# A two-layer mixer on one core: 128-column token sums at the start, wider lead groups with the last one's modulation on VectorE, and token-major last output columns

## The chip, the core and the metric

The kernel runs on one NeuronCore of one Trainium2 chip. The metric is the time of one launch on the device, in microseconds (us), as the median of several runs; lower is better. The engines are called PE (TensorE, the matrix engine), DVE (VectorE), ACT (ScalarE), POOL (GpSimd) and SP (SyncE, which here only issues DMAs). All of a core's engines run their own instruction streams in order and wait for one another through semaphores.

## The reference, cut to what matters

Context tokens (128) and sample tokens (256) go through two layers and a final norm. `cvec` is one conditioning vector for the context tokens and another for the sample tokens.

```python
def trunk_layer(x, cvec, l, p, ...):
    shift, scale, gate = jnp.split(jax.nn.silu(cvec) @ p['w_mod'][l] + p['b_mod'][l], 3, axis=-1)
    h = rmsnorm(x, p['norm_g'][l]) * (1 + scale) + shift
    (f_x, f_g, p_x, p_g, q, k, v, a_g, c_a, c_b, c_g) = jnp.split(h @ p['w_in'][l], 11, axis=-1)
    ...                                   # four mixers, each multiplied by silu of its gate
    y = jnp.concatenate([y_f, y_p, y_a, y_c], axis=-1) @ p['w_out'][l]
    return x + gate * y, k, v
y = rmsnorm(x, final_g)                   # after the second layer
```

`x` has 384 tokens of 2048 channels; `w_mod[l]` is 2048 x 6144, `w_in[l]` 2048 x 5632, `w_out[l]` 2048 x 2048, all in fp32.

## The kernel before

**Layout.** Activations stand channel-major: 16 blocks of 128 channels on the partitions, 384 tokens along the free dimension. Every large product is made of three single-pass products (`mm3`, lines 439 to 442): the weight and the activation are each split into a rounded part and a rest (`hi`, `lo` of a weight tile; `hh`, `hl` of `h`; `yh`, `yl` of the mixers' output), and hi x hi, hi x rest and rest x hi are added in PSUM. `wtile` (line 227) loads a weight tile `raw` by DMA (512 KB for two channel blocks and 512 output columns), copies it rounded to `hi` on ACT and subtracts to `lo` on DVE.

**The start.** Three dummy products (`idle`, line 167) on a zero tile `still` stand ahead. The tokens' sums of squares over all channels come from `token_sums` (line 421): the squared channels are the stationary operand and one column of ones is the moving one. From the sums come 1/rms (`rstd_cols`), its diagonal, and a broadcast product `bc`; from `h`'s scale and shift (`AB`) and `bc`, `make_h` (line 427) makes a channel block of `h` with four DVE and two ACT instructions. The scale and shift are the product of `silu(cvec)` with columns of `w_mod`; `mod_item` (line 255) does it on PE, with the two conditioning vectors as stationary operand in 32 columns (`cmod`), four column strips side by side, from 512 KB tiles `mraw` in the pool `Y`.

**The lead phase.** `h` isn't ready at once, so four of layer 0's input chunks (`C_B`, `C_A`, `K_`, `Q_`, 512 columns each) run group by group over the channel blocks: `groups` are two of one block and seven of two. Within a group each of the four chunks takes all four PSUM tiles of the pool `mmp`, runs `main_tile` (24 products of 384 columns for two blocks) and leaves a partial result, which DVE adds to `acc[ci]` in four instructions (helper `tt`, line 107); the next chunk on PE needs those PSUM tiles back. The modulation of the next group (`mod_group`, eight `mod_item`s) is put ahead of the first and the third chunk, and `make_h` for the next group ahead of the fourth. PE and SP follow the written order throughout this phase, DVE and ACT the order that the scheduler makes.

**The end.** In layer 1, `w_out` is applied for four groups of 512 output channels. `finish_block` (line 914) adds gate times result to `x`, squares it and adds the squares to `sacc`. The first three groups are multiplied by `final_g`, transposed to token-major on PE and copied to `ot`. The fourth group runs one block of 128 channels at a time; only after its last block are the token sums complete, 1/rms known, and twelve tiles of 128 tokens x 512 channels scaled and stored.

Of the kernel before, what the change touches and what calls it, by code (L numbers as in the profile page):

```python
# [8 lines left out]
F32 = mybir.dt.float32  # L9
# [5 lines left out]
P = 128  # L15
# [40 lines left out]
def mixer_step(  # L56
    ctx: ExitStack,
    tc: tile.TileContext,
    x_in, cache_k, cache_v, consts, lam, packs,
# [76 lines left out]
    nc.vector.memset(still, 0.0)  # L136
# [3 lines left out]
    nc.vector.memset(cmod, 0.0)  # L140

# [17 lines left out]
    act(warm, cmod[:, 0, 2:3], AF.Sqrt, bias=eps_t[:, 0:1])  # L159
# [183 lines left out]

    fill = {"pe": [], "dve": []}
# [76 lines left out]
    def token_sums(st, acc, start=True, stop=True):  # L421
        for t in range(TB):
            nc.tensor.matmul(st[:, t:t + 1], lhsT=acc[:, t * P:(t + 1) * P], rhs=ones[:, 0:1], start=start and t == 0,  # L423
                             stop=stop and t == TB - 1)
        return st[:, 0:TB]
# [358 lines left out]
    for l in range(DEPTH):  # L784
        if l == 0:
            groups = [(0, 1), (1, 1)] + [(k, 2) for k in range(2, KC, 2)]
            first = mod_group(0, *groups[0])
            ssq = sm("ssq")
            for g in range(4):
                if g == 3:  # L790
                    for it in first[:2]:
                        mod_item(*it)
                for i in range(2):
                    stat = token_sums(ssq, xsq[g][:, i, :], g == 0 and i == 0, g == 3 and i == 1)
            dg = diagonal(rstd_cols(stat, TB, 1.0 / D))
# [8 lines left out]
        hh = [gtile("H", "hh", dt=F32R) for _ in range(4)]  # L804
        hl = [gtile("H", "hl", dt=F32R) for _ in range(4)]
        res = {}
        if l == 0:
# [106 lines left out]
        def finish_block(g, b, ps, outs):  # L914
# [18 lines left out]
        otk = []  # L933
        for g in range(4):
            ps4 = [mmp.tile([P, 512], F32, tag="mm", name=nm("mm")) for _ in range(4)]
# [6 lines left out]
            for b in range(4):  # L942
                if g == 3:
                    c0 = g * BR + b * P
                    for k0 in range(0, KC, 8):
# [6 lines left out]
                        if b == 3 and k0 == 0:  # L952
                            tots.append(mdp.tile([P, 512], F32, tag="md", name=nm("st")) if final else sm("st"))
# [4 lines left out]
            elif g < 3:  # L958
# [147 lines left out]
```

## Time and profile before

| | us |
|---|---|
| median of 3 runs | 1249.11 |
| runs | 1248.88 to 1251.1 |
| the profiled execution, its time | 1249.6 |
| the profiled execution, its span | 1247.8 |
| mean granted PE clock (share of full speed) | 0.986 |

The span runs from the first to the last recorded instruction; 1.8 us of the profiled time lie around it. Shares of busy time are averages over stages; the rows further down are read stage by stage. All times in rows are us from the span's start unless marked ns.

### The profile page before, as it was taken

Reading aid. Unit: us, or ns where it says so; the run is one execution under the profiler, and the core shown is the slowest. Engines: PE = TensorE matmul, PEld = TensorE weight load, DVE = VectorE, ACT = ScalarE, POOL = GpSimd, SP = SyncE. Lnnn points to the kernel's source line nnn. Section 1 sums busy time; section 2 is a strip of 40 time slices with the busy share of each in tenths; the row PEclk is TensorE's granted clock in tenths of the full one; section 3 lists DMA queues with packets and bytes.
Section 4 is the critical chain, followed back from the end, with each engine's and each line's share of the span. In section 5 each row is a group of like instructions: output and inputs, shape, how many; then the busy total and the mean of one; then the engine's idle time right before and its main releaser. Section 6 shows DMA issues by size and latency. Waiting matters only on the chain.

```text
span 1247.8 us, 22061 instructions
## 1 busy us (share of the span) xinstructions
PE 1223.0 (98%) x8558; PEld 1148.6 (92%) x8558; DVE 922.4 (74%) x1774; ACT 550.3 (44%) x1103; POOL 2.1 (0%) x34
## 2 busy tenths in 40 slices
PE   8999999999999999999999999999999999999995
PEld 6899998898999999999998999989999999999995
DVE  4787879999957956989968469997464895647452
ACT  3433333444547644433335433334455755344442
POOL 0000000000000000000000000000000000000000
PEclk6999999999999999999999999999999999999998
DMA  8988886553346766988945444444232563645322
GB/s 302 351 314 318 304 306 236 171 175 122 132 169 218 281 228 221 330 302 319 326 155 185 161 152 161 152 163 156 80 101 102 194 228 118 211 152 186 119 68 101
DMA packets 70712, 251.85 MB, mean 202 GB/s; under 512 B 7760, under 2 KB 8912, under 8 KB 70608
## 3 DMA queue, kind: packets, MB, share of 16 engines
q1 hardware_dynamic: 70608, 250.45, 57.1%
q8 instruction: 67, 1.10, 0.4%
q14 instruction: 37, 0.30, 0.1%
HBM read 243.08 MB, written 7.34 MB: 201 GB/s over the span
## 4 chain that ended last, share of the span: by engine, by line
PE 91%; DVE 5%; DMA 1%; ACT 1%; issue 1%; SPq 0%; DVEq 0%; ACTq 0%
PE mm L440 24%; PE mm L442 23%; PE mm L441 23%; PE mod L279 5%; PE mm L471 2%; PE mm L472 2%; PE mm L473 2%; DVE lo L107 1%; PE sp L440 1%; PE sp L441 1%; PE sp L442 1%; DVE cacc L110 1%; PE fb L712 1%; PE ssq L423 1%; PE aso L669 1%
## 5 line engine op out<-in xcount | busy, mean ns | idle before, releaser
L116 ACT ACTIVATE hi<-raw 128x512 fp32r<-128x512 f32 x498 | 308.9, 631 | 532.6 <-PE mm L441 345.8
L107 DVE TENSOR_TENSOR lo<-raw,hi 128x512 fp32r<-128x512 f32 x498 | 336.8, 688 | 212.7 <-ACT hi L116 203.6
L440 PE MATMUL mm<-hh,hi 128*128 128x384 f32 x1280 | 441.0, 345 | 3.7 <-ACT hh L113 3.7
L442 PE MATMUL mm<-hh,lo 128*128 128x384 f32 x1280 | 433.0, 338 | 2.5 <-DVE lo L107 2.5
L441 PE MATMUL mm<-hl,hi 128*128 128x384 f32 x1280 | 433.0, 338 | 0.0
L440 PEld LDWEIGHTS mm<-hh,hi 128*128 128x128 f32 x1280 | 242.0, 189 | 23.6 <-issue 10.1
L442 PEld LDWEIGHTS mm<-hh,lo 128*128 128x128 f32 x1280 | 242.3, 189 | 3.5 <-DVE lo L107 3.4
L441 PEld LDWEIGHTS mm<-hl,hi 128*128 128x128 f32 x1280 | 242.4, 189 | 1.0 <-DVE hl L110 0.4
L440 PE MATMUL mm<-yh,hi 128*128 128x384 f32 x512 | 173.6, 341 | 0.6 <-DVE xr L110 0.6
L441 PE MATMUL mm<-yl,hi 128*128 128x384 f32 x512 | 172.6, 337 | 0.0
L442 PE MATMUL mm<-yh,lo 128*128 128x384 f32 x512 | 172.5, 338 | 0.0
L110 DVE SCALAR_TENSOR_TENSOR macc<-sraw,cmod,macc 128x512 f32<-128x512 f32 x210 | 147.6, 746 | 6.3 <-DMA sraw<-in_w_mod_dram 6.3
L110 DVE SCALAR_TENSOR_TENSOR cacc<-u,cst,cacc 128x399 f32<-128x399 f32 x232 | 146.5, 631 | 6.0 <-ACT cacc L113 1.5
L440 PEld LDWEIGHTS mm<-yh,hi 128*128 128x128 f32 x512 | 96.4, 188 | 4.1 <-issue 2.5
L441 PEld LDWEIGHTS mm<-yl,hi 128*128 128x128 f32 x512 | 96.5, 188 | 0.0
L442 PEld LDWEIGHTS mm<-yh,lo 128*128 128x128 f32 x512 | 96.4, 188 | 0.0
L107 DVE TENSOR_TENSOR acc<-acc,mm 128x384 f32<-128x384 f32 x128 | 66.5, 553 | 26.9 <-PE mm L442 26.6
L279 PE MATMUL mod<-mraw,cmod 128*32 128x128 f32 (+2 forms) x1920 | 74.7, 296 | 0.0
L279 PEld LDWEIGHTS mod<-mraw,cmod 128*32 128x32 f32 x1920 | 49.7, 114 | 18.5 <-issue 10.6
L113 ACT ACTIVATE hh<-ht,AB 128x128 fp32r<-128x128 f32 x64 | 27.2, 451 | 27.5 <-DVE ht L110 26.8
L471 PE MATMUL mm<-hi,hh 128*128 128x512 f32 x96 | 38.3, 399 | 0.0
L472 PE MATMUL mm<-lo,hh 128*128 128x512 f32 x96 | 38.0, 396 | 0.0
(211 smaller groups left out, 944.0 us busy)
## 6 DMA issues: line engine op xcount, KB each, us to landing
raw<-in_w_in_dram SPq DMA_DIRECT2D x172, 512.0 KB, 4.2
mraw<-in_w_mod_dram SPq DMA_DIRECT2D x136, 512.0 KB, 4.6
raw<-in_w_out_dram SPq DMA_DIRECT2D x64, 512.0 KB, 4.2
sraw<-in_w_mod_dram SPq DMA_DIRECT2D x56, 512.0 KB, 5.6
xT<-in_x_dram SPq DMA_DIRECT2D x4, 768.0 KB, 6.8
xr<-in_x_dram SPq DMA_DIRECT2D x4, 768.0 KB, 6.5
xd<-xr SPq DMA_DIRECT2D x4, 768.0 KB, 5.1
xr<-xd SPq DMA_DIRECT2D x4, 768.0 KB, 5.8
```

The lines of the kernel that those rows point to most:

```text
L107: (eng or nc.vector).tensor_tensor(out=out, in0=a, in1=b, op=op)
L110: nc.vector.scalar_tensor_tensor(out=out, in0=a, scalar=s, in1=b, op0=op0, op1=op1)
L113: nc.scalar.activation(out=out, in_=a, func=func, **kw)
L116: nc.scalar.activation(out=out, in_=a, func=AF.Copy, scale=scale)
L279: nc.tensor.matmul(ps[qs, 0:nb * 32].rearrange("p (b n) -> p b n", n=32), lhsT=cmod[:, k0 + j, :], rhs=raw[:, j, :, qs], start=(k0 + j == ...
L423: nc.tensor.matmul(st[:, t:t + 1], lhsT=acc[:, t * P:(t + 1) * P], rhs=ones[:, 0:1], start=start and t == 0, stop=stop and t == TB - 1)
L440: nc.tensor.matmul(ps, lhsT=wh, rhs=ah, start=start, stop=False)
L441: nc.tensor.matmul(ps, lhsT=wh, rhs=al, start=False, stop=False)
L442: nc.tensor.matmul(ps, lhsT=wl, rhs=ah, start=False, stop=stop)
L471: nc.tensor.matmul(ps3[t], lhsT=hh[g][:, kb, ts], rhs=hi(j), start=st, stop=False)
L472: nc.tensor.matmul(ps3[t], lhsT=hh[g][:, kb, ts], rhs=lo(j), start=False, stop=False)
L473: nc.tensor.matmul(ps3[t], lhsT=hl[g][:, kb, ts], rhs=hi(j), start=False, stop=sp)
```

## The change

Four parts.

1. `token_sums` takes a width `n`; at the start the moving operand is 128 columns of ones in place of one. The first two `mod_item`s, which stood between the third and the fourth tile's sums on PE, now stand behind all the sums; three items follow the sums and the fourth follows the broadcast product. The zero tile is written by POOL in place of DVE, and the load of the square root's table on ACT moves behind the first squares.
2. The lead groups are (0,1), (1,1), (2,2), (4,2), (6,2), (8,4), (12,4), written as first block and number of blocks: seven in place of nine. A group of four blocks keeps its PSUM tiles over two weight tiles, so it has one round of additions to `acc` for four blocks.
3. The modulation of blocks 12 to 15 leaves PE's `mod_item`s. `lead_item(k)` loads a tile `lraw` with 128 rows of `w_mod` and the 1024 columns of shift and scale of those blocks, and DVE adds it, times each of the two conditioning values, to two accumulators `lacc` of 128 x 1024. One item stands in each chunk from group 1 on, sixteen in all, so in groups 1 to 4. After the sixteenth, eight products with `pick` sum over the partitions on PE, and DVE transposes and stores.
4. The last 512 output channels are computed token-major: the activations are stationary and 512 columns of `w_out` move, first for the context tokens and the first 128 sample tokens over all eight weight tiles, then for the last 128 sample tokens, over three tiles still held and five loaded and split again. Gate and `x` are transposed to token-major ahead. Each block of tokens has its own sum, root, scaling and four stores.

```diff
     still = gtile("H", "still", (P, 512))
-    nc.vector.memset(still, 0.0)
+    nc.gpsimd.memset(still, 0.0)
...
+    def lead_item(k, accs):
+        if k == 0:
+            accs.extend(gtile("H", "lacc", (P, 8, P)) for _ in range(2))
+        raw = gtile("Y", "lraw", (P, 2, 512))
...
+        nc.sync.dma_start(out=raw, in_=packs["w_mod"].take(rows, (P, 2, 512)))
+        src = raw.rearrange("p s n -> p (s n)")
+        for v in range(2):
+            a = accs[v].rearrange("p b n -> p (b n)")
+            cv = cmod[:, k, v:v + 1]
+            if k == 0:
+                nc.vector.tensor_scalar(out=a, in0=src, scalar1=cv, scalar2=None, op0=ALU.mult)
+            else:
+                stt(a, src, cv, a, ALU.mult, ALU.add)
+        if k == KC - 1:
+            ps = sm("lmd", (P, 8, 32))
+            for q in range(4):
+                qs = slice(32 * q, 32 * q + 32)
+                for v in range(2):
+                    nc.tensor.matmul(ps[qs], lhsT=pick[:, v, :], rhs=accs[v][:, :, qs], start=v == 0, stop=v == 1)
...
-            groups = [(0, 1), (1, 1)] + [(k, 2) for k in range(2, KC, 2)]
+            groups = [(0, 1), (1, 1), (2, 2), (4, 2), (6, 2), (8, 4), (12, 4)]
...
-                if g == 3:
-                    for it in first[:2]:
-                        mod_item(*it)
                 for i in range(2):
-                    stat = token_sums(ssq, xsq[g][:, i, :], g == 0 and i == 0, g == 3 and i == 1)
+                    stat = token_sums(ssq, xsq[g][:, i, :], g == 0 and i == 0, g == 3 and i == 1, P)
             dg = diagonal(rstd_cols(stat, TB, 1.0 / D))
-            for it in first[2:]:
+            for it in first[:3]:
                 mod_item(*it)
...
         bc_ps = bcast_tokens(dg)
+        if l == 0:
+            mod_item(*first[3])
...
+                    if gi and by_dve:
+                        by_dve -= 1
+                        lead_item(LEAD_DVE - 1 - by_dve, lead_acc)
+                    if c >= 2 and not last and (c == 3 or len(pairs) > 1):
+                        k, n = pairs[c - 2] if len(pairs) > 1 else pairs[0]
+                        more_h((k + n + 3) // 4)
+                        make_h(0, xT, bc, range(k, k + n), hh, hl)
+                    for i, ks in enumerate(tiles):
+                        main_tile(ps4, *ws[i], ks, hh, hl, i == 0, i + 1 == len(tiles))
...
+    def tokens_tile(w, kt, ts, first, last):
...
+            for t in ts:
...
+                nc.tensor.matmul(ps3[t], lhsT=ah, rhs=hi(j), start=first and j == 0, stop=False)
+                nc.tensor.matmul(ps3[t], lhsT=ah, rhs=lo(j), start=False, stop=False)
+                nc.tensor.matmul(ps3[t], lhsT=al, rhs=hi(j), start=False, stop=last and j == 1)
+
+    def finish_tokens(t):
+        z = xt[:, t, :]
+        tt(zt[:, t, :], ps3[t], gb[:, min(t, 1), :], ALU.mult)
+        tt(z, zt[:, t, :], z, ALU.add)
+        act(zt[:, t, :], z, AF.Square, accum_out=own[:, t:t + 1])
+        s = tiny.tile([P, 1], F32, tag="sqt", name=nm("sq"))
+        act(s, own[:, t:t + 1], AF.Sqrt, scale=1.0 / D, bias=rest[:, t:t + 1])
+        r = tiny.tile([P, 1], F32, tag="rst", name=nm("rs"))
+        nc.vector.reciprocal(out=r, in_=s)
+        for g in range(4):
...
+            nc.sync.dma_start(out=dst, in_=ots[g][:, t, :] if g < 3 else z)
...
+    for i, kt in enumerate(order):
+        ws.append(wtile(srcs[i]))
+        tokens_tile(ws[i], kt, (0, 1), i == 0, i == 7)
+    for t in (0, 1):
+        finish_tokens(t)
+    again = (5, 6, 7, 0, 1, 2, 3, 4)
+    for n, i in enumerate(again):
+        w = ws[i] if n < 3 else wtile(srcs[i])
+        tokens_tile(w, order[i], (2,), n == 0, n == 7)
+    finish_tokens(2)
```

Three places show what moves. On PE at the program's start, before (`idle` are the dummy products, `ssq` the token sums, `mod` the modulation, `bc` the broadcast, `mm` the first main product):

```order
L167 MATMUL idle_138<-still_111,ones 128x512 x3
L423 MATMUL ssq_163<-ones,xsq_7_142 128x1 x6
L423 MATMUL ssq_163<-ones,xsq_8_146 128x1 x6
L423 MATMUL ssq_163<-ones,xsq_9_150 128x1 x6
L279 MATMUL mod_184<-mraw_182,cmod 32x64 x16
L279 MATMUL mod_184<-mraw_201,cmod 32x64 x16
L423 MATMUL ssq_163<-ones,xsq_10_154 128x1 x6
L279 MATMUL mod_184<-mraw_231,cmod 32x64 x16
L279 MATMUL mod_184<-mraw_249,cmod 32x64 x16
L418 MATMUL bc_272<-dg_229,ones 128x384
L440 MATMUL mm_298<-hh_275,hi_285 128x384
```

and in the changed kernel, the same place on PE:

```order
L170 MATMUL idle_141<-still_111,ones 128x512 x3
L460 MATMUL ssq_167<-ones,xsq_7_145 128x128 x6
L460 MATMUL ssq_167<-ones,xsq_8_150 128x128 x6
L460 MATMUL ssq_167<-ones,xsq_9_154 128x128 x6
L460 MATMUL ssq_167<-ones,xsq_10_158 128x128 x6
L284 MATMUL mod_200<-mraw_198,cmod 32x64 x16
L284 MATMUL mod_200<-mraw_217,cmod 32x64 x16
L284 MATMUL mod_200<-mraw_235,cmod 32x64 x16
L455 MATMUL bc_253<-dg_196,ones 128x384
L284 MATMUL mod_200<-mraw_255,cmod 32x64 x16
L477 MATMUL mm_300<-hh_279,hi_287 128x384
```

The sums are 128 columns wide and stand together, and one modulation item stands behind the broadcast.

On DVE in lead group 2 (blocks 2 and 3), from the additions of its second chunk (`acc_378`) to those of its third (`acc_446`), before (`T` and `AB` are the small transposes and additions of a modulation, `ht` the first step of `make_h`):

```order
L107 TENSOR_TENSOR acc_378<-acc_378,mm_775 128x384
L284 STREAM_TRANSPOSE T_868<-mod_705 128x128
L107 TENSOR_TENSOR AB_159<-T_868,cst 128x2x2
L107 TENSOR_TENSOR T_868<-T_868,cst 128x2x2
L107 TENSOR_TENSOR lo_908<-raw_905,hi_907 128x512
L110 SCALAR_TENSOR_TENSOR AB_159<-T_868,cst 128x2x2
L107 TENSOR_TENSOR lo_912<-raw_905,hi_911 128x512
L110 SCALAR_TENSOR_TENSOR ht_915<-xT_124,AB_159,bcs_274 128x128
L110 SCALAR_TENSOR_TENSOR ht_915<-xT_124,AB_159,bcs_274 128x256
L110 SCALAR_TENSOR_TENSOR ht_922<-xT_124,AB_159,bcs_274 128x128
L107 TENSOR_TENSOR acc_446<-acc_446,mm_814 128x384
```

and in the changed kernel on DVE, in the same group, from the last addition of the first chunk (`acc_316`) to those of the second (`acc_380`) and what follows them:

```order
L107 TENSOR_TENSOR acc_316<-acc_316,mm_712 128x384
L110 SCALAR_TENSOR_TENSOR lacc_538<-lraw_810,cmod,lacc_538 128x1024
L107 TENSOR_TENSOR lo_803<-raw_800,hi_802 128x512
L107 TENSOR_TENSOR lo_807<-raw_800,hi_806 128x512
L110 SCALAR_TENSOR_TENSOR lacc_539<-lraw_810,cmod,lacc_539 128x1024
L107 TENSOR_TENSOR lo_849<-raw_846,hi_848 128x512
L107 TENSOR_TENSOR lo_853<-raw_846,hi_852 128x512
L107 TENSOR_TENSOR acc_380<-acc_380,mm_796 128x384
L107 TENSOR_TENSOR acc_380<-acc_380,mm_797 128x384
L107 TENSOR_TENSOR acc_380<-acc_380,mm_798 128x384
L107 TENSOR_TENSOR acc_380<-acc_380,mm_799 128x384
L110 SCALAR_TENSOR_TENSOR lacc_538<-lraw_901,cmod,lacc_538 128x1024
```

Two instructions of 128 x 1024 stand between the additions of every two chunks.

On DVE at the end, from the last block's addition of gate times result on, before (`rs` is 1/rms of all tokens, `ot` and `otp` the outputs to be scaled):

```order
L110 SCALAR_TENSOR_TENSOR xr_11507<-mm_12529,GT_162,xr_11507 128x128
L110 SCALAR_TENSOR_TENSOR xr_11507<-mm_12529,GT_162,xr_11507 128x256
L407 RECIPROCAL rs_12849<-sq_12847 128x3
L982 TENSOR_SCALAR res_12851<-ot_11848,rs_12849 128x512 x2
L982 TENSOR_SCALAR res_12858<-ot_12203,rs_12849 128x512 x2
L982 TENSOR_SCALAR res_12865<-ot_12522,rs_12849 128x512
```

and on DVE in the changed kernel, from the first two token blocks' products (`zt`) to the last weight rest of the second pass (`rs` are 1/rms of a token block, `ot` the earlier groups' outputs):

```order
L107 TENSOR_TENSOR zt_12418<-mm_12419,gb_12374 128x512
L107 TENSOR_TENSOR zt_12418<-mm_12420,gb_12374 128x512
L107 TENSOR_TENSOR xt_12392<-zt_12418,xt_12392 128x512 x2
L107 TENSOR_TENSOR lo_12649<-raw_12646,hi_12648 128x512
L107 TENSOR_TENSOR lo_12653<-raw_12646,hi_12652 128x512
L107 TENSOR_TENSOR lo_12665<-raw_12662,hi_12664 128x512
L107 TENSOR_TENSOR lo_12669<-raw_12662,hi_12668 128x512
L107 TENSOR_TENSOR lo_12681<-raw_12678,hi_12680 128x512
L107 TENSOR_TENSOR lo_12685<-raw_12678,hi_12684 128x512
L107 TENSOR_TENSOR lo_12697<-raw_12694,hi_12696 128x512
L1079 RECIPROCAL rs_12603<-sq_12601 128x1
L1084 TENSOR_SCALAR ot_11696<-ot_11696,rs_12603 128x512
```

The five reloaded tiles' rests and the finishing of two token blocks share DVE during the second pass.

## Rows read from the trace of the kernel before

**Rows 1.** The page's first part: busy time and share of the span by engine.

```profile
PE 1223.0 (98%) x8558; PEld 1148.6 (92%) x8558; DVE 922.4 (74%) x1774; ACT 550.3 (44%) x1103; POOL 2.1 (0%) x34
```

**Rows 2.** Stretches (start:end, length, busy by engine, PEclk, DMA share, GB/s): lead groups.

```profile
37.90:116.20 78.30, 75.84 (x853) 71.14 (x856) 63.96 (x145) 25.91 (x49) 0.00 (x0) 1.00 0.89 334
116.20:201.20 85.00, 84.56 (x843) 78.50 (x844) 66.87 (x151) 27.61 (x52) 0.00 (x0) 1.00 0.83 308
```

**Rows 3.** The chain that ended last, lead phase: start, us, what.

```profile
74.50 1.88 PE mod L279 x64
...
116.18 1.93 PE mod L279 x64
```

**Rows 4.** Groups of DVE instructions, 37.9 to 116.2: busy, mean ns | idle before.

```profile
L107 DVE TENSOR_TENSOR acc<-acc,mm 128x384 f32<-128x384 f32 x63 | 32.8, 553 | 11.5 <-PE mm L442 11.3
...
L110 DVE SCALAR_TENSOR_TENSOR hl<-ht,AB,hh 128x128 fp32r<-128x128 f32 (+1 forms) x16 | 6.1, 415 | 0.3 <-ACT hh L113 0.3
```

**Rows 5.** Stretches of the start, columns as in rows 2.

```profile
9.00:10.00 1.00, 1.00 (x6) 1.00 (x6) 1.00 (x2) 0.31 (x1) 0.00 (x0) 0.50 1.03 430
...
29.00:30.00 1.00, 1.00 (x62) 0.87 (x64) 0.06 (x1) 0.48 (x1) 0.00 (x0) 0.93 0.00 0
```

**Rows 6.** The start in order of time, PE and one DVE row.

```profile
1.59 4.64 PE L167 MATMUL idle<-still,ones 128*128 128x512 f32 x6 [1.59 <-DVE still L136]
8.00 7.27 PE L423 MATMUL ssq<-ones,xsq 128*128 128x1 f32 x36 [1.77 <-DVE xsq L107]
...
12.79 0.96 DVE L107 TENSOR_TENSOR xsq<-xsq 128x768 f32<-128x768 f32 x1
...
19.71 1.93 PE L279 MATMUL mod<-mraw,cmod 128*32 128x64 f32 x64
21.58 1.65 PE L418 MATMUL bc<-dg,ones 128*128 128x384 f32 x2
24.60 0.69 PE L440 MATMUL mm<-hh,hi 128*128 128x384 f32 x1 [1.37 <-ACT hh L113]
...
29.14 1.08 PE L279 MATMUL mod<-mraw,cmod 128*32 128x64 f32 x61
```

**Rows 7.** The end in order of time: PE, ACT, DVE and SP.

```profile
1233.20 0.34 PE L442 MATMUL mm<-yh,lo 128*128 128x384 f32 x1
...
1235.80 0.26 ACT L113 ACTIVATE sq<-st,eps_t 128x3 f32<-128x3 f32 x1 [0.27 <-PE st L423]
...
1236.31 2.07 DVE L982 TENSOR_SCALAR res<-ot,rs 128x512 f32<-128x512 f32 x5
...
1236.82 7.24 SPq L987 DMA_DIRECT2D out_dram<-res  x12
```

**Rows 8.** PE in order of time: token-major products, and fp32 products of 128 columns.

```profile
201.16 0.39 PE L471 MATMUL mm<-hi,hh 128*128 128x512 f32 x1
...
201.85 0.39 PE L471 MATMUL mm<-hi,hh 128*128 128x512 f32 x1
...
298.11 2.84 PE L712 MATMUL fb<-cst,u 128*128 128x128 f32 x24
```

**Rows 9.** DVE in order of time: start, us, what; instructions back to back.

```profile
53.25 1.94 DVE L107 TENSOR_TENSOR acc<-acc,mm 128x384 f32<-128x384 f32 x4
55.11 2.49 DVE L107 TENSOR_TENSOR lo<-raw,hi 128x512 fp32r<-128x512 f32 x4
...
203.12 1.22 DVE L107 TENSOR_TENSOR rm<-acc,cst 128x1024 f32<-128x1024 f32 x1
204.25 1.22 DVE L107 TENSOR_TENSOR rsh<-rsh,cst 128x1024 f32<-128x1024 f32 x1
...
400.23 4.72 DVE L110 SCALAR_TENSOR_TENSOR macc<-sraw,cmod,macc 128x512 f32<-128x512 f32 x7
```

**Rows 10.** Groups of DVE instructions of the modulation on DVE, whole span.

```profile
L110 DVE SCALAR_TENSOR_TENSOR macc<-sraw,cmod,macc 128x512 f32<-128x512 f32 x210 | 147.6, 746 | 6.3 <-DMA sraw<-in_w_mod_dram 6.3
...
L329 DVE TENSOR_SCALAR macc<-sraw,cmod 128x512 f32<-128x512 f32 x14 | 6.2, 481 | 3.2 <-DMA sraw<-in_w_mod_dram 3.2
```

More of the change, by code (lines that the diff above doesn't have):

```diff
@@ L140, in mixer_step @@
     nc.vector.memset(cmod, 0.0)
+    pick = one.tile([P, 2, 32], F32, tag="pick", name="pick")
+    nc.gpsimd.memset(pick, 0.0)
+    for v in range(2):
+        nc.gpsimd.memset(pick[:, v, v:v + 1], 1.0)
     in_order = ExitStack()
@@ L419, in bcast_tokens, with token_sums @@
         return bc
[L421 removed]
+    def token_sums(st, acc, start=True, stop=True, n=1):
         for t in range(TB):
[L423 to L425 removed]
+            nc.tensor.matmul(st[:, t * n:(t + 1) * n], lhsT=acc[:, t * P:(t + 1) * P], rhs=ones[:, 0:n],
+                             start=start and t == 0, stop=stop and t == TB - 1)
+        return st[:, 0:TB] if n == 1 else st[:, 0:TB * n].rearrange("p (t n) -> p t n", n=n)[:, :, 0]
     def make_h(l, xT, bc, kcs, hh, hl):
@@ L803, in mixer_step, with more_h @@
             copy_a(bc, bc_ps[:, :NT])
-        hh = [gtile("H", "hh", dt=F32R) for _ in range(4)]
-        hl = [gtile("H", "hl", dt=F32R) for _ in range(4)]
+        hh, hl = [], []
+        def more_h(n):
+            while len(hh) < n:
+                hh.append(gtile("H", "hh", dt=F32R))
+                hl.append(gtile("H", "hl", dt=F32R))
+        more_h(4 if l else 3)
         res = {}
@@ new lines, in mixer_step @@
+    gb = gtile("H", "gb", (P, 3, BR))
+    nc.sync.dma_start(out=gb[:, 2, :], in_=final_b)
+    for v in range(2):
+        gw = gtile("H", "gw", (P, 4, P))
+        nc.vector.tensor_copy(out=gw, in_=GT[l][:, 4 * G:4 * G + 4, v].unsqueeze(2).to_broadcast([P, 4, P]))
+        ps = sm("gbp")
+        for b in range(4):
+            nc.tensor.transpose(ps[:, b * P:(b + 1) * P], gw[:, b, :], ident)
+        nc.scalar.copy(out=gb[:, v, :], in_=ps)
+    xt = gtile("H", "xt", (P, TB, BR))
+    for t in range(TB):
+        ps = sm("xtp")
+        for b in range(4):
+            nc.tensor.transpose(ps[:, b * P:(b + 1) * P], xT[G][:, b, t * P:(t + 1) * P], ident)
+        nc.scalar.copy(out=xt[:, t, :], in_=ps)
@@ new lines, in mixer_step @@
+    rest = tiny.tile([P, TB], F32, tag="rest", name="rest")
+    part = token_sums(mdp.tile([P, 512], F32, tag="md", name="st"), sacc)
+    nc.vector.tensor_scalar(out=rest, in0=part, scalar1=1.0 / D, scalar2=EPS, op0=ALU.mult, op1=ALU.add)
+    own = tiny.tile([P, TB], F32, tag="own", name="own")
+    zt = gtile("H", "zt", (P, TB, BR))
+    def tokens_tile(w, kt, ts, first, last):
+        hi, lo = w
+        for j in range(2):
+            kc = 2 * kt + j
+            for t in ts:
+                ah = yh[kc // 4][:, kc % 4, t * P:(t + 1) * P]
+                al = yl[kc // 4][:, kc % 4, t * P:(t + 1) * P]
+                nc.tensor.matmul(ps3[t], lhsT=ah, rhs=hi(j), start=first and j == 0, stop=False)
+                nc.tensor.matmul(ps3[t], lhsT=ah, rhs=lo(j), start=False, stop=False)
+                nc.tensor.matmul(ps3[t], lhsT=al, rhs=hi(j), start=False, stop=last and j == 1)
```

80 lines of the change are left out of this document (51 added, 29 removed).

## The prediction, made before the changed kernel ran

> **What bounds the kernel now.** The busy shares came first: PE works 98% of the span, DVE 74% [rows 1]. So a change gains only where it shortens PE's own list or a place where PE stands still, and it loses where it makes another engine the slower one for a stretch. The change touches three stretches, and each was then read by itself.
>
> *Lead phase.* In the windows of lead groups 1 to 4 and 5 to 8, PE is busy 75.84 of 78.30 us and 84.56 of 85.00; DVE is busy 63.96 and 66.87 [rows 2]. On the chain of waits the modulation sets of two successive groups begin 74.50 and 116.18: two groups, so one takes 20.84 us [rows 3]. It holds two sets of 1.88 us and 4 x 24 = 96 products, hence (20.84 - 3.76) / 96 = 0.178 us for each product. DVE's idle time there is mostly the 11.5 us ahead of the additions to `acc`, and PE's product ends it [rows 4]. PE sets the pace and DVE has some 14 us to spare in 78.
>
> *Start.* PE runs at a granted clock of 0.50 between 9 and 10 us, which is the 1.2 GHz level, and has 0.93 between 29 and 30 [rows 5]. At the low level lie the dummy products, the sums, both modulation sets and the broadcast; the first main product starts at 24.60 [rows 6].
>
> *End.* The last product starts 1233.20 and ends 1233.54. Then come the last addition, square, sums and root; the root starts 1235.80, and twelve stores are issued from 1236.82 for 7.24 us, 0.6 each, until 1244.06 [rows 7]. The span ends at 1247.8: 14.3 us after the last product, of which 3.7 follow the last issue.
>
> **The start: -5.1 (from -6 to +3.2).** A 128-column sum is on the chip's record elsewhere: 24 instructions of `fb`, fp32 and 128 columns, took 2.84, so 0.118 each [rows 8]. A tile of sums is twelve: 1.4. The last squares end at 12.79 + 0.96 = 13.75 [rows 6], which sets the earliest end of the sums; if PE keeps up it is 15.2, against 19.7 before, when two modulation items (1.93) stood in between and PE was slow. Whether it keeps up is the clock's question. Wide products give PE real streaming work where one-column sums gave it little, and I take it that the clock rises. The later modulation set at the high clock takes 1.08 for 61 instructions, 0.0177 each [rows 6]: three items, 96 instructions, 1.7, to 16.9; the broadcast at half of 1.65, 0.8; the fourth item 0.55; 18.2. Before, from the end of the last modulation (19.71 + 1.93 = 21.64) to the first main product went 2.96 through ACT and DVE, which have no TensorE clock, so I keep it: 21.2 in place of 24.60, -3.4. From there the first chunk's twelve products and their waits took 29.14 - 24.60 = 4.5; at 0.178 they are 2.1, with 0.7 of waits left 2.8: -1.7. If the clock stays low, 48 sums at 0.236 are 11.3 and end at 19.3, three items at 0.030 end at 22.2, broadcast and fourth item at 24.8, the first product at 27.8: +3.2. The zero tile on POOL and the moved table load cost nothing, since the squares of the last tile come later; without that cover, a microsecond.
>
> **The lead phase: +14.8 (from +9 to +23).** Removed: the eight PE items for blocks 12 to 15 and, from the merged groups, half of their rounds of additions. Added on DVE in groups 1 to 4: sixteen `lead_item`s of two 1024-column instructions. No row has that shape; two bound it. The `macc` instruction, same operation at 512 columns, has a pace of (4.72 - 0.746) / 6 = 0.662 [rows 9]; twice that, 1.32, is the upper end. 1024 columns of a two-source addition follow each other by 204.25 - 203.12 = 1.13 [rows 9], the lower end. Between them I take the same operation's 0.662 and let the further 512 columns cost what additions pay from 384 (0.465 apiece, 1.86 / 4 [rows 9]) to 1024: (1.13 - 0.465) / 640 = 1.04 ns a column, 0.53, together 1.195. Thirty at 1.195 and two first ones at 0.75 (481 ns at 512 columns for the one-source form [rows 10]): 37.4.
>
> The Trainium skill, "Vector Engine (DVE) Microarchitecture Reference", section "Measured stream behaviour on trn2 (trn3 not measured)", gives about 1.04 ns a column plus about 75 ns, an estimate of 1.14 for such an instruction; the addition of 1024 columns (1.13) agrees, the `macc` pace (0.662, where the rule gives 0.608) doesn't. By it the sum would be 1.6 lower, about 1253.5.
>
> DVE's list for groups 1 to 4 is then 64.0 + 37.4. A next group of four blocks wants eight more `ht` and `hl` there, at about 0.38 [rows 4]: +3.1. And `acc` additions, when they needn't wait for PE, follow each other at 0.465 in place of 0.52 (32.8 / 63) [rows 4, 9]: 64 of them, -3.5. Together 101. PE's list there stays 75.84 plus the `pick` products. So for these groups the bound moves from PE to DVE. PE can't run ahead: each chunk takes all four PSUM tiles, and the additions that free them stand on DVE behind two `lacc` instructions. Behind those wait also the weight rests `lo` of the next chunks. DVE in its turn will still wait now and then (a chunk's first addition for its last product, `hl` for ACT, the last item for its load): before, such waits other than for `acc` were under 3 us; I add 5. So 106 in place of 78.3: +27.7, between 101 with the cheap shape (+21) and 113 with the dear one and more waiting (+34.5).
>
> Behind that, groups 5 and 6 hold the same 384 products as groups 5 to 8 had, with two modulation sets left of eight: 384 x 0.178 + 3.76 = 72.1 against 85.0, -12.9. DVE has half the additions there and isn't the bound. 27.7 - 12.9 = +14.8.
>
> **The end: -3.5 (from -5.5 to +1).** Token-major main products of 512 columns: three in 201.85 - 201.16 = 0.69 [rows 8], 0.2333 with rounding over more of them; 144 of them are 33.6, against 192 x 0.178 = 34.2 for the last group before. The transposes of gate and `x` and their copies lie ahead, beside PE's work but partly on it: +1. After the last product now come two DVE instructions of 512 columns at about 0.69, a square with its sum at 0.85, root 0.26, reciprocal and scaling some 0.8 with handing over, and four stores at 0.6: 5.9, then 3.7 [rows 7]: 9.6 against 14.3, -4.7. The sums' products and the transposed 1/rms go. The second pass is nearly full on DVE: ten rests at 2.49 / 4 = 0.62 [rows 9] and finishing two token blocks, 5.5, are 11.7, while PE's 48 products take 11.2. The stores of the first two blocks lie under that pass.
>
> **Sum.** -5.1 + 14.8 - 3.5 = +6.2. The profiled execution's time is 1249.6, 0.5 above the median; it would become 1255.8, and the median 1255. About 0.2%, 2.5 us, is what a measurement of this kernel can tell from no change.
>
> **Rivals.**
>
> *The clock stays low until the main products, 13 in 100.* Against it: the sums become wide. For it: weight loads were busy 1.00 of the window at 0.50 clock already [rows 5], so busy PE alone didn't raise it, and PE still stands idle 1.77 after the dummies [rows 6]. The start is then +3.2 in place of -5.1: 1263. The Trainium skill, "TensorE: Matmul & The Clock Gate", section "Why this matters for your kernels", says that gaps between products cost the clock; the start's gap would remain, and no row here says which side wins.
>
> *The lead products cost what a one-source instruction does, 9 in 100, the faster side.* Then 32 x 0.75 = 24 in place of 37.4, DVE's list is 88, and the sum is -7.2: 1242. The change wins once the instruction costs under about 0.95. Against it: 210 `macc` take 746 ns, the one-source form 481 at equal columns [rows 10]. The Trainium skill, "VectorE: DVE Perf Modes", section "Mode 2×_2P — use both read ports for one tensor", gives the doubled rate to one-source operations alone, and these two rows agree.
>
> *DMA becomes the bound of the lead, 12 in 100.* At 0.89 busy and 334 GB/s [rows 2] the queues are near full, and sixteen `lraw` tiles are moved forward. Chunks of four blocks hold two weight tiles, so group 4's stretch orders some 24 transfers of 524 KB: 12.6 MB, 37.7 us at 334 GB/s, against DVE's some 29. +8: 1263. For it is the high share; against it, that the longer stretch of groups 1 to 3 lets loads run ahead.
>
> *No difference, 12 in 100.* DVE's list comes out at its low end and hides its waits: start -6, lead +10, end -5: -1, about 1248 to 1250.
>
> *The second pass is starved, 10 in 100.* If the five reloaded tiles come late or DVE's two lists collide, PE waits for `lo`: the end is +1, not -3.5: 1259.5.
>
> **Chances.** The forecast 44 in 100; the rivals as given. The range from 1247 to 1265 leaves out the faster rival and the joint bad ends. Most cases lie on one side: faster by over 0.2% has 12 in 100 (the cheap lead products, some of the favourable ends), within 0.2% 11, slower 77.
>
> **What would show it.** The start: a granted clock near full from 10 to 15 us, the first main product near 21. The lead: DVE busy nearly throughout groups 1 to 4, PE's idle time ended by `acc` additions, those groups about 106 us and the last two about 72; `lacc` at about 1.2. If PE's idle is ended by weight or `lraw` loads instead, the DMA rival holds; if PE doesn't idle there, my list for DVE is too long. The end: the last store issued about 6 us after the last product, and PE waiting little for `lo` in the second pass.

## The result, and the profile after

The changed kernel takes 1262.68 us (median of 4 runs, 1261.21 to 1266.07) against 1248.99 for the kernel before, a ratio of 1.011 with a 95% interval of 1.0087 to 1.0133: 13.7 us slower where 6 were forecast. The profiled execution's span is 1260.5 us, 12.7 longer than before; the working below goes by the two spans.

The page's first part of the changed kernel, which answers to [rows 1]:

```profile
PE 1218.0 (97%) x8272; PEld 1131.0 (90%) x8272; DVE 947.7 (75%) x1781; ACT 556.8 (44%) x1116; POOL 2.7 (0%) x38
```

PE has 5 us less work and the span is 12.7 longer, so PE stands still for some 18 us more. The stretches tell where. These are the changed kernel's lead groups 1, 2, 3 and 4, the four together, and groups 5 and 6 (columns as in [rows 2]; the bounds are the last main product of each group):

```profile
33.80:56.20 22.40, 16.09 (x178) 14.09 (x176) 17.56 (x30) 4.30 (x10) 0.00 (x0) 0.85 0.90 322
56.20:81.70 25.50, 21.64 (x225) 19.73 (x224) 25.23 (x46) 6.58 (x13) 0.00 (x0) 1.00 0.89 333
81.70:106.70 25.00, 21.93 (x227) 19.78 (x225) 25.00 (x46) 6.19 (x13) 0.00 (x0) 1.00 0.92 348
106.70:145.10 38.40, 29.99 (x370) 24.05 (x369) 33.69 (x74) 12.44 (x24) 0.00 (x0) 0.91 0.90 343
33.80:145.10 111.30, 89.65 (x994) 77.66 (x993) 101.48 (x192) 29.51 (x57) 0.00 (x0) 0.94 0.90 338
...
145.10:218.60 73.50, 73.28 (x460) 68.51 (x459) 54.86 (x113) 26.07 (x46) 0.00 (x0) 1.00 0.62 209
```

and the kernel before, groups 1 to 4 one by one:

```profile
37.80:52.90 15.10, 13.04 (x177) 11.51 (x176) 10.84 (x27) 5.49 (x11) 0.00 (x0) 1.00 0.95 344
52.90:74.40 21.50, 21.10 (x225) 19.80 (x224) 18.46 (x42) 6.77 (x13) 0.00 (x0) 1.00 0.92 363
74.40:95.20 20.80, 20.80 (x225) 19.92 (x224) 17.14 (x38) 7.62 (x15) 0.00 (x0) 1.00 0.84 312
95.20:116.10 20.90, 20.90 (x225) 19.87 (x224) 17.43 (x42) 6.14 (x11) 0.00 (x0) 1.00 0.88 318
```

All four groups are longer, the fourth most (38.4 against 20.9). DVE is busy 101.5 of 111.3 and the DMA engines 0.90 at 338 GB/s: neither has much left. By group, DVE stands idle for 4.8, 0.3, 0.0 and 4.7. The waits there of PE, then of DVE (what waited for what: us, times, longest):

```profile
PE mm L479 <- DVE lo L107: 14.2, 8, 3.3
PE mod L284 <- DMA mraw<-in_w_mod_dram: 4.1, 6, 1.3
PE lmd L375 <- DVE lacc L110: 2.7, 2, 2.6
PE mm L477 <- DVE acc L107: 0.5, 2, 0.3
...
DVE acc L107 <- PE mm L479: 4.1, 3, 3.1
DVE T L289 <- PE mod L284: 4.0, 3, 2.5
```

Most of PE's waits end with a weight's rest `lo`, and one of them shows what stands behind it. These are rows of ACT, DVE and PE in lead group 1, in order of time:

```profile
39.24 0.63 ACT L116 ACTIVATE hi<-raw 128x512 fp32r<-128x512 f32 x1 [1.89 <-DMA raw<-in_w_in_dram]
...
39.95 1.27 DVE L110 SCALAR_TENSOR_TENSOR lacc<-lraw,cmod,lacc 128x1024 f32<-128x1024 f32 x1
41.14 0.68 DVE L107 TENSOR_TENSOR lo<-raw,hi 128x512 fp32r<-128x512 f32 x1
...
41.88 0.44 PE L479 MATMUL mm<-hh,lo 128*128 128x384 f32 x1 [3.26 <-DVE lo L107]
...
48.61 2.48 DVE L110 SCALAR_TENSOR_TENSOR lacc<-lraw,cmod,lacc 128x1024 f32<-128x1024 f32 x2
```

ACT waits for the weight tile to land; when it has, DVE is within a lead instruction, and `lo` comes behind it. PE's 3.26 us are one wait with two causes, a late load and a busy DVE. (The last row, two lead instructions back to back, is used further down.)

The start of the changed kernel, by stretches, then the same two stretches of the kernel before:

```profile
10.00:12.00 2.00, 1.67 (x13) 1.48 (x13) 1.90 (x3) 0.94 (x2) 0.00 (x0) 1.00 1.00 410
12.00:14.00 2.00, 1.67 (x13) 1.48 (x14) 1.68 (x2) 0.53 (x1) 0.00 (x0) 1.00 1.04 422
...
18.30:21.00 2.70, 0.06 (x5) 0.02 (x1) 2.52 (x9) 1.48 (x4) 0.00 (x0) 1.00 1.02 394
...
22.00:25.00 3.00, 3.00 (x11) 2.74 (x9) 0.59 (x1) 1.92 (x4) 0.00 (x0) 0.52 1.03 399
```

```profile
10.00:12.00 2.00, 2.00 (x11) 2.00 (x11) 1.90 (x3) 0.94 (x2) 0.00 (x0) 0.50 1.01 412
12.00:14.00 2.00, 2.00 (x11) 2.00 (x11) 1.64 (x2) 0.44 (x1) 0.00 (x0) 0.50 1.02 412
```

With 128 columns the granted clock holds at 1.00 through the sums; PE even waits a little. Then PE stands still from 18.3 to 21. The clock is still 1.00 in that wait and until 22; from 22 to 25 it is 0.52 (the 1.2 GHz level). PE in order of time, which answers to [rows 6]:

```profile
13.84 1.60 PE L460 MATMUL ssq<-ones,xsq 128*128 128x128 f32 x12 [0.33 <-DVE xsq L107]
...
20.98 0.44 PE L477 MATMUL mm<-hh,hi 128*128 128x384 f32 x1 [2.64 <-ACT hh L113]
...
23.12 0.53 PE L477 MATMUL mm<-hh,hi 128*128 128x384 f32 x1
23.45 0.53 PE L478 MATMUL mm<-hl,hi 128*128 128x384 f32 x1
...
25.18 1.25 PE L284 MATMUL mod<-mraw,cmod 128*32 128x64 f32 x64
```

The first main product comes at 20.98, 3.6 earlier than before, but the first chunk's products follow each other at 0.33 us and it lasts until 25.18.

The end, PE, ACT and SP, which answers to [rows 7]:

```profile
1250.96 0.39 PE L1069 MATMUL mm<-hi,yl 128*128 128x512 f32 x1
...
1253.72 0.29 ACT L113 ACTIVATE sq<-own,rest 128x1 f32<-128x1 f32 x1
...
1254.76 1.30 SPq L1090 DMA_DIRECT2D out_dram<-ot  x3
...
1256.15 0.40 SPq L1090 DMA_DIRECT2D out_dram<-xt  x1
```

The last product ends at 1251.35, the last store is issued by 1256.55, and the span ends at 1260.5: 9.15 us after the last product in place of 14.3.

### The profile page after: what moved, and what is told of

Same layout as the page of the kernel before. It is cut to its first block, busy times and chain, and to the rows that moved or that the text cites. A ratio compares the mean times of both kernels' runs of the same rounds, so it can differ in the third digit from the quotient of the medians.

```text
span 1260.5 us, 21544 instructions
## 1 busy us (share of the span) xinstructions
PE 1218.0 (97%) x8272; PEld 1131.0 (90%) x8272; DVE 947.7 (75%) x1781; ACT 556.8 (44%) x1116; POOL 2.7 (0%) x38
## 5 line engine op out<-in xcount | busy, mean ns | idle before, releaser
L107 DVE TENSOR_TENSOR lo<-raw,hi 128x512 fp32r<-128x512 f32 x508 | 344.9, 688 | 229.2 <-ACT hi L116 215.2
L479 PE MATMUL mm<-hh,lo 128*128 128x384 f32 x1280 | 433.7, 339 | 14.2 <-DVE lo L107 14.2
L477 PE MATMUL mm<-yh,hi 128*128 128x384 f32 x448 | 151.7, 340 | 1.5 <-DVE xr L110 1.3
L479 PE MATMUL mm<-yh,lo 128*128 128x384 f32 x448 | 150.7, 337 | 0.0
L478 PE MATMUL mm<-yl,hi 128*128 128x384 f32 x448 | 150.6, 336 | 0.0
L477 PEld LDWEIGHTS mm<-yh,hi 128*128 128x128 f32 x448 | 84.1, 188 | 5.1 <-issue 4.0
L478 PEld LDWEIGHTS mm<-yl,hi 128*128 128x128 f32 x448 | 84.3, 188 | 0.0
L479 PEld LDWEIGHTS mm<-yh,lo 128*128 128x128 f32 x448 | 84.1, 188 | 0.0
L284 PEld LDWEIGHTS mod<-mraw,cmod 128*32 128x32 f32 x1664 | 41.7, 111 | 24.8 <-issue 11.6
L107 DVE TENSOR_TENSOR acc<-acc,mm 128x384 f32<-128x384 f32 x96 | 47.5, 548 | 4.2 <-PE mm L479 4.1
L510 PE MATMUL mm<-hi,hl 128*128 128x512 f32 x96 | 38.0, 395 | 0.0
```

The source lines that it names most:

```text
L107: (eng or nc.vector).tensor_tensor(out=out, in0=a, in1=b, op=op)
L284: nc.tensor.matmul(ps[qs, 0:nb * 32].rearrange("p (b n) -> p b n", n=32), lhsT=cmod[:, k0 + j, :], rhs=raw[:, j, :, qs], start=(k0 + j == ...
L477: nc.tensor.matmul(ps, lhsT=wh, rhs=ah, start=start, stop=False)
L478: nc.tensor.matmul(ps, lhsT=wh, rhs=al, start=False, stop=False)
L479: nc.tensor.matmul(ps, lhsT=wl, rhs=ah, start=False, stop=stop)
L510: nc.tensor.matmul(ps3[t], lhsT=hl[g][:, kb, ts], rhs=hi(j), start=False, stop=sp)
```

## The experiments

Two theories of the lead phase stood against each other. **DVE:** its list of some 101 us in groups 1 to 4 sets their length, as the forecast had it. **Loads:** the sixteen `lraw` tiles (8.4 MB), and eight more `mraw` tiles (4.2 MB) that group 4 needs for the next group's second pair of blocks, come on top of 26 MB in a stretch where the DMA engines were 0.89 busy already. Beside these, start and end were taken apart. The runs were made in three rounds, in which the kernel before measured 1250.01, 1249.57 and 1250.16; differences below between runs of two rounds carry that half microsecond.

**Start and end without the lead change.** In the changed kernel:

```diff
-    LEAD_DVE = KC
+    LEAD_DVE = 0
...
-            groups = [(0, 1), (1, 1), (2, 2), (4, 2), (6, 2), (8, 4), (12, 4)]
+            groups = [(0, 1), (1, 1)] + [(k, 2) for k in range(2, KC, 2)]
...
-                        if k < 12:
-                            nxt += mod_group(0, k, n)
+                        nxt += mod_group(0, k, n)
```

> The changed kernel with the lead phase of before: nine groups, all modulation on PE; the new start and the token-major end stay. If the three parts of the change add up, start -3.8, end -3.6 and the wait for `pt` that went (-1.1) are left, and the lead phase is as before: 1249 - 7.4 to - 8.5, so 1240.5 to 1241.6. Rival: the start's gain is swallowed in lead group 1, where loads were at 0.95 of the DMA engines before and can't come earlier: then some 1244.5 to 1245.5, and group 1 is 3 to 4 us longer than the 15.1 of before.

Measured: 1242.4 us against 1250.01, ratio 0.9939 (0.9925 to 0.9952). The span is 1239.8, 8.0 shorter than before. Groups 1 to 4 together:

```profile
33.60:111.80 78.20, 75.89 (x850) 71.12 (x849) 63.47 (x145) 26.36 (x51) 0.00 (x0) 1.00 0.91 338
```

They take what they took before [rows 2] and begin some 4 us earlier, so the start's gain isn't swallowed there. The whole loss of the change is the lead change's: some 20 us.

**The new start alone.** The kernel before, with the 128-column sums, the order of the start, the zero tile on POOL and the moved table load.

> The kernel before with the new start alone (128-column sums, their order, the zero tile on POOL, the table load moved); old lead, old end. By the two traces the start is worth 24.60 - 20.98 = 3.6, or 3.8 by lead group 1: 3.5 to 4.2 us faster than before. The rest of the 7.6 to 8.0 that start and end gave together is then the end's 3.6 and the vanished wait of 1.1. If the end's part is nothing without the other, this kernel is 6 us or more faster.

Measured: 1246.35 against 1250.16, ratio 0.9976 (0.9965 to 0.9986), -3.8. The rest of the 7.6 is the end's; start and end add up.

**The new start with narrow sums.**

```diff
-                    stat = token_sums(ssq, xsq[g][:, i, :], g == 0 and i == 0, g == 3 and i == 1, P)
+                    stat = token_sums(ssq, xsq[g][:, i, :], g == 0 and i == 0, g == 3 and i == 1)
```

> New start, old lead, new end, but the token sums with one moving column instead of 128, in the new order (all modulation behind the sums). If the width is what keeps TensorE's clock up, the granted clock falls to 0.50 within the sums as in the kernel before, 48 sums take 0.20 to 0.23 each and end near 18.2 instead of 15.2, three modulation items and the broadcast cost 1.5 to 2 us more, and the first main product comes at 24.5 to 26 instead of 20.8: 4 to 5 us slower than 1242.4. Rival: the order alone gains the time (the modulation no longer stands between the sums), and the time is within 1 us of 1242.4.

Measured: 1246.36, 4.0 slower than with wide sums, ratio to before 0.9973 (0.9963 to 0.9982). Two stretches, then the first main product:

```profile
12.00:14.00 2.00, 2.00 (x12) 2.00 (x11) 1.90 (x3) 0.66 (x1) 0.00 (x0) 0.50 1.03 416
14.00:18.00 4.00, 4.00 (x20) 4.00 (x20) 0.16 (x1) 0.00 (x0) 0.00 (x0) 0.50 1.04 402
```

```profile
25.81 0.47 PE L477 MATMUL mm<-hh,hi 128*128 128x384 f32 x1 [2.64 <-ACT hh L113]
```

The clock is 0.50 while PE and its weight loads are busy all the time, and the first product comes 5.0 later (25.81 against 20.80). The width does it; the new order alone gives nothing.

**PE's idle stretch filled.** In the kernel with start and end alone, three dummy products (`FILL` is 3) ahead of the first main one:

```diff
             mod_item(*first[3])
+        if l == 0:
+            for _ in range(FILL):
+                nc.tensor.matmul(idle, lhsT=ones, rhs=still, start=True, stop=True)
```

> As the kernel with old lead, new start and new end, with three dummy products of 512 columns on PE between the fourth modulation item and the first main product, where PE stood idle for 2.64 us. If that idle time is why the first chunk's products ran at 0.32 us apiece, they now run at 0.17 to 0.18 and the twelve take 2.1 instead of 3.9: about 1.0 to 1.5 us faster than the kernel without the dummies, unless loads of the second chunk come no earlier. Rival: the first chunk waits for weights anyway, and the time is the same within 0.3 us. If the dummies outlast the wait, it is slower by up to 0.5.

Measured: 1239.86, ratio to before 0.9919 (0.9905 to 0.9932); 2.5 below the kernel without the dummies by the medians, 1.3 by the spans (1238.5 and 1239.8); by the means it is 2.3, with a 95% interval of some 1.6 either way. The stretch in which the clock had been 0.52, and products of the first chunk:

```profile
21.00:25.00 4.00, 3.73 (x78) 3.07 (x77) 1.41 (x4) 2.62 (x7) 0.00 (x0) 1.00 1.04 406
```

```profile
22.23 0.34 PE L478 MATMUL mm<-hh,hi 128*128 128x384 f32 x1
22.41 0.34 PE L479 MATMUL mm<-hl,hi 128*128 128x384 f32 x1
...
23.89 1.10 PE L285 MATMUL mod<-mraw,cmod 128*32 128x64 f32 x64
```

The clock stays at 1.00, products follow at 0.17 to 0.18, and the chunk ends at 23.89. So it was after the idle 2.64 us, and because of them, that the clock had fallen. This kernel is the fastest of all that were run.

**Half of the lead's DVE work.** In the changed kernel:

```diff
-            else:
+            elif v == 0:
                 stt(a, src, cv, a, ALU.mult, ALU.add)
```

> The changed kernel; the second conditioning vector's accumulation is left out after the first item, so that 15 of the 32 instructions of 1024 columns are gone from DVE in groups 1 to 4, with all loads kept. Theory DVE: its list of 101 us sets the pace of these groups; less 15 x 1.20 = 18 the list is 83, the groups take about 93 in place of 110.7, the time falls by 15 to 18, to 1245 to 1248. Theory loads: the sixteen extra transfers set the pace; the groups stay above 105 and the time falls by less than 6, above 1256.

Measured: 1256.49, -6.2. Groups 1 to 4:

```profile
33.60:138.40 104.80, 87.16 (x994) 76.09 (x993) 86.19 (x173) 28.06 (x55) 0.00 (x0) 0.97 0.92 350
```

18 us of lead work less on DVE (its busy time falls by 15.3) bring 6.5, and DVE now stands idle for 18.6. The theory that DVE alone sets the pace falls.

**All lead loads left out.**

```diff
-        raw = gtile("Y", "lraw", (P, 2, 512))
...
-        nc.sync.dma_start(out=raw, in_=packs["w_mod"].take(rows, (P, 2, 512)))
-        src = raw.rearrange("p s n -> p (s n)")
+        packs["w_mod"].take(rows, (P, 2, 512))
+        src = xT[k % 4].rearrange("p b n -> p (b n)")[:, 0:1024]
```

> The changed kernel; the sixteen `lraw` loads are left out, and the accumulations read the tokens `xT` that lie in SBUF in place of rows of `w_mod`; all DVE work is kept. Theory DVE: groups 1 to 3 stay within 2 us of 72.8 and only group 4 loses its waits for `mraw` (4.1): the time falls by 3 to 6, to 1257 to 1260. Theory loads: all four groups shorten, together by 15 or more, and the time falls to below 1249.

Measured: 1244.96, -17.7. Groups 1 to 4:

```profile
34.20:130.30 96.10, 84.73 (x995) 76.16 (x993) 92.33 (x181) 28.32 (x56) 0.00 (x0) 0.98 0.80 300
```

Groups 1 and 2 are back at 15.5 and 21.8, and DVE is now busy 92 of 96. For these two the run isn't clean: without a load to wait for, the scheduler put the first items into group 0, so eight of the 32 lead instructions, some 9 us of DVE work, left them. Groups 3 and 4 keep their eight each, and there the loads can be read by themselves: 24.4 and 34.4 without them, 25.0 and 38.4 with them.

**Loads kept, nearly no lead work on DVE.**

```diff
+            if k:
+                a, src = a[:, 0:32], src[:, 0:32]
```

> The changed kernel; from the second lead item on DVE adds only 32 of the 1024 columns, so that the sixteen `lraw` loads stay and 15 x 2 x 1.1 = 33 us of DVE work are gone. Theory loads (the transfers of groups 1 to 4, some 38 MB, take 105 to 111 us at the 338 to 350 GB/s seen there): these groups stay above 98 us and the time above 1249. Theory DVE: DVE's list is some 70, PE's 85, the groups take 85 to 90 and the time falls below 1242. Halving the DVE work left 104.8 of 111.3 with DVE idle for 18, so I expect 98 to 103.

Measured: 1254.25, -8.4. Groups 1 to 4, then what the DMA engines moved in them:

```profile
33.60:134.70 101.10, 85.77 (x994) 75.38 (x993) 73.68 (x188) 27.26 (x55) 0.00 (x0) 0.98 0.95 364
```

```profile
DMA packets 10294, 36.82 MB, mean 364 GB/s; under 512 B 1146, under 2 KB 1146, under 8 KB 10283
```

With DVE 27 us short of full, the groups still take 101, and all four are longer than before: 36.8 MB at 364 GB/s, the engines 0.95 busy. So the loads lengthen these groups without DVE's lead work, to about the length of DVE's list. That the rate alone does it isn't shown: over the stretches of the start shown above, the engines moved 394 to 422 GB/s, at which 36.8 MB would take some 90 us (an estimate), and SP, which issues the loads, waits here for DVE for some 30 us.

**Buffers of their own for the lead loads.** `lraw` leaves the pool `Y` for the buffer `cvp` (every second item) and two of `kvp`:

```diff
-        raw = gtile("Y", "lraw", (P, 2, 512))
...
+        if k % 2 == 0:
+            raw = cvtile("lraw").rearrange("p a b -> p (a b)")[:, 0:1024]
...
+        else:
+            parts = []
+            for s in range(2):
+                raw = kvp.tile([P, 512], F32, tag="kv", name=nm("lraw"))
+                nc.sync.dma_start(out=raw, in_=src[:, s, :])
+                parts.append((raw, 512 * s, 512 * s + 512))
```

> The changed kernel, with `lraw` in buffers that nothing else uses in the lead phase (one of 1024 columns and two of 512) in place of the pool `Y`, which it shares with the modulation tiles `mraw`; every second item is then four DVE instructions of 512 columns, +2 us of DVE work in all. If loads are late because SP's queue stands still for a free buffer of `Y`, groups 1 to 4 fall from 111.3 to 101 to 104 (DVE's list), the time to 1252 to 1255. If the transfer rate itself is the limit, the groups stay within 3 us of 111.3, the time at 1259 to 1265.

Measured: 1261.25; groups 1 to 4 take 110.6 in place of 111.3. So it isn't the sharing of the pool `Y` that makes the loads late. It doesn't clear SP's queue, though, which issues in the written order. SP's longest waits in groups 1 to 4, in the kernel before, in the changed kernel, and in this one:

```profile
SPq L271 <- PE mod L279: 46.8, 16, 7.3
...
SPq L361 <- DVE lacc L110: 22.7, 6, 5.0
SPq L361 <- DVE ht L110: 14.2, 3, 5.2
...
SPq L369 <- DVE lacc L110: 20.9, 8, 5.6
```

Before, SP waited for PE's modulation and for DVE for 3 us in all. In the changed kernel it waits for DVE for 62 us, and with the other buffers, each of which comes round again after two items, still for 52. From 63.9 to 69.05, for one, the changed kernel's SP issues nothing, and the DMA engines run short of work (0.66 busy) while DVE is busy throughout:

```profile
64.00:70.00 6.00, 3.78 (x23) 3.46 (x22) 6.00 (x10) 1.15 (x2) 0.00 (x0) 1.00 0.66 269
```

So some loads are issued late because DVE is late in giving buffers back, just as DVE's `lo` is late because of loads. What this is worth beside the transfer rate, no run separates.

**The merging alone.** New start and end, groups of the changed kernel, `LEAD_DVE = 0` and all modulation on PE.

> New start and end, groups of four blocks, all modulation on PE: the merging alone, against the kernel with the old lead (1242.4). Theory loads: group 4 has to bring sixteen `mraw` (8.4 MB) and the eight weight tiles of group 5 (4.2 MB), at 345 GB/s 36 us less what is loaded early; it takes 31 to 36 in place of 20.8, and the time is 1249 to 1254. Theory DVE: with no additions on DVE group 4 takes PE's 24.6 and the merged rest costs nothing, the time is 1241 to 1244.

Measured: 1246.77, 4.4 slower than the kernel with the old lead. Group 4, groups 1 to 4, and the rest of the lead:

```profile
91.00:118.00 27.00, 25.55 (x354) 23.02 (x353) 19.54 (x51) 7.90 (x18) 0.00 (x0) 1.00 0.94 357
33.60:118.00 84.40, 80.70 (x978) 74.27 (x977) 65.78 (x154) 27.88 (x56) 0.00 (x0) 1.00 0.92 346
118.00:200.80 82.80, 81.31 (x717) 74.97 (x715) 57.54 (x123) 26.95 (x49) 0.00 (x0) 1.00 0.77 284
```

Between the two expectations: group 4 takes 27.0, of which 25.6 are PE's own work, with two modulation sets more than before. Waits add 1.5 us, not ten; group 3 moved only 306 GB/s, so there was room to load ahead, which may be why. The rest is 2.1 us shorter than with the old groups (82.8 against 84.9).

**The DVE modulation alone, in groups of before.**

```diff
-            groups = [(0, 1), (1, 1), (2, 2), (4, 2), (6, 2), (8, 4), (12, 4)]
+            groups = [(0, 1), (1, 1)] + [(k, 2) for k in range(2, KC, 2)]
```

> New start and end, nine groups of before, the modulation of blocks 12 to 15 on DVE in groups 1 to 4: the other half alone. Both theories give groups 1 to 4 about 101 to 106 (8.4 MB more at 345 GB/s are 24 us on 78.2; DVE's list is 63.5 + 37.4 = 101), with group 4 at about 26 instead of 38.4; the later groups lose four modulation sets, 84.8 - 7.5 = 77. Time 1242.4 + 25 - 7.5 = 1258 to 1262, about what the whole change has. If group 4 stays above 32, the extra `mraw` of a wide group isn't what lengthens it.

Measured: 1261.44, 19 slower than without the DVE modulation, and within 1.3 of the whole change. Groups 1 to 4 take 106.3, group 4 of them 33.4, not 26:

```profile
106.50:139.90 33.40, 25.86 (x242) 21.89 (x241) 29.85 (x60) 11.14 (x21) 0.00 (x0) 0.90 0.84 315
```

So in that group the wide next group explains 5 us (38.4 against 33.4); the rest of its length is that of the lead items and their loads.

## Why the prediction was wrong

The terms of its sum, by the two profiled executions:

| term | forecast | measured |
|---|---|---|
| start, to lead group 1 | -5.1 | -3.8 |
| lead groups 1 to 4 | +27.7 | +33.0 (111.3 against 78.3) |
| groups 5 and 6 for 5 to 8 | -12.9 | -11.7 |
| between lead and end | 0 | -1.2 |
| end | -3.5 | -3.6 |
| sum | +6.2 | +12.7 |

*The lead groups 1 to 4* are the step that failed. Much of its working held: a lead instruction's pace is 1.20 (2.48 for two less 1.28 for one, forecast 1.195), DVE's work in these groups is 101.5 (forecast 101), and in groups 2 and 3 DVE is busy throughout, as forecast (25.23 of 25.50 and 25.00 of 25.00). Mis-sized was "I add 5" for DVE's waits, read from a trace in which DVE was not the bound, with the extra transfers at nothing in the sum; they were weighed as a rival that takes the bound over, in group 4 alone. DVE stood idle for 9.8, nearly all of it in groups 1 and 4 and in waits for PE, which itself waited for `lo` and for `mraw`. With the lead loads left out DVE's idle time was 3.8, so without them 5 was about right. Four runs, all with the new start, the new end and the wide groups, set the two lists side by side (the one with neither has this modulation on PE, in group 5):

| groups 1 to 4 | no lead work on DVE | lead work on DVE |
|---|---|---|
| no lead loads | 84.4 | 96.1 (9 us of it moved ahead) |
| lead loads | 101.1 | 111.3 |

Neither list by itself nor both additions together (some 122) is the answer. With the 9 us back, the kernel without lead loads would take about 105 (an estimate: 92 busy, 9 moved, 4 idle); so the loads cost some 6 on top of DVE's work, and DVE's work 10 on top of the loads. Groups 3 and 4, where nothing had moved, agree: the loads cost 0.6 and 4.0 there. The waiting product at 41.88 shows how they meet: a weight tile lands late, and then its rest queues behind a lead instruction; and SP's waits show the way back, buffers that DVE gives back late. The clock has a part too: PE's own work in these groups is 89.65 at a granted clock of 0.94, and 80.70 at 1.00 in the run with all modulation on PE, which has the same products there but for those with `pick`. How much of the time each of the three costs wasn't taken apart.

The DMA rival, at 1263, came close to the measured time partly by luck: the loads lengthen all four groups and add to DVE's list, where the rival had them take over from DVE in group 4 for 8 us; in that group they cost 4. The rival in which the lead products cost 0.75 is refuted by their pace of 1.20. Of the named signs, PE's idle time was to be ended by `acc` additions; 0.5 us of it was, and 14.2 by `lo`.

*The start.* The first product at 20.98 (forecast 21.2) and the held clock were right. "At 0.178 they are 2.1" was not: a microsecond after that product the clock fell, and the first chunk took 4.2 in place of 2.8. The forecast named the gap after the dummies as a danger and overlooked the other, 2.64 us ahead of the first product, that its own working kept. The Trainium skill, "TensorE: Matmul & The Clock Gate", section "Why this matters for your kernels", warns that gaps between products cost the clock; the filled gap agrees with it (0.52 without, 1.00 with the dummies). A slip beside it: the dummy products were put at the low clock, but the clock of before is 1.00 there (1.6 to 6.2) and falls within the sums, to 0.83 from 8 to 9 and 0.50 from 9 to 10.

*Groups 5 and 6* were mis-sized by 1.2. PE hardly waits there (73.28 busy of 73.50); beside the two modulation sets counted, further instructions of the gate's modulation stand in the last chunks, at 208.80, 210.08 and 218.13.

*Between lead and end* nothing was forecast. In the kernel before, PE waits once for the attention weights; the waits of PE there:

```profile
PE fa L692 <- ACT pt L113: 1.1, 1, 1.1
```

In the changed kernel that wait is gone. It is there at 1.1 in every run with nine lead groups, and gone or at 0.3 in those with groups of four. So it belongs to the merging; through what, wasn't followed.

*The end* came out near: 9.15 after the last product (forecast 9.6), and 1.5 more of products and transposes ahead of it. The forecast's -3.5 leaves 1.2 for the latter, of which its text works out only 0.4 (33.6 for 34.2, and 1 for transposes), so that part is a hit without a working.

*Slips of the working* that change nothing above: the terms of the 5.9 after the last product add to 5.7; 101 less 78.3 is 22.7, not 21; the change breaks even at lead instructions of about 0.99, not 0.95 (6.2 less over thirty); and PE's list in group 4 was said to stay, though the next group of four puts two more modulation sets there, 3.8 us, which PE had to spare.

## What to carry to other kernels

Work that is moved to an idle engine brings its transfers along: cost the stretch it moves into by bytes as well as by instructions, and when two lists there are about as long as each other, expect more than the longer one (here 111, for some 105 and 101), since each can be late because of the other: DVE for a load, and a load for a buffer that DVE holds. A wait of TensorE just ahead of its main work cost twice here, once itself and once in the clock after it; products on data that lay there already were a cheap cover. Parts of a change should be costed and tried one by one: two of these four were worth 8 us, and were buried under 20.

## What the runs showed of the hardware

- That PE is busy did not hold its clock: with one moving column the granted clock was 0.50 where PE and its weight loads were busy all the time (4.00 of 4.00), with 128 columns 1.00 where PE was busy 1.67 of 2.00.
- An idle stretch of 2.64 us was followed, a microsecond after it, by some 3 us at 0.52; with dummies of about 2.7 us in it the clock stayed at 1.00.
- Over 100 us, transfers of 512 KB reached 364 GB/s with the DMA engines 0.95 busy; 334 GB/s at 0.89, as before, was within a tenth of that. In stretches of 2 to 4 us of the start it was 394 to 422.
- A SCALAR_TENSOR_TENSOR on VectorE of 1024 fp32 columns has a pace of 1.20 us back to back, and 0.66 at 512 columns [rows 9].
